# The S5 recurrence as rotations by tables around two scans, and the SSD gate's sums on another engine

## The chip, the cores and the metric

The program runs on one core of a Trainium2 chip. The metric is the device time of one execution in microseconds (us); the median of three runs counts. The profile is of one further execution of the same program. Engines: TensorE (PE) for matmuls, VectorE (DVE), ScalarE (ACT), GpSimd (POOL), and SyncE (SP), which issues most of the transfers. Each engine takes its instructions strictly in the order of its own queue and waits on semaphores for the others.

## The reference

The model has two blocks; the change is in the first, which has two layers (DEPTH = 2) with a mixer each, for 256 tokens of width 1024. A mixer projects its input, runs an SSD branch (chunks of 128 tokens, 32 heads) and an S5 branch, and merges them by gates. All is float32. The part that matters here is the S5 branch, a diagonal complex recurrence in 64 groups of 16 channels and 64 states:

```python
lam_bar = jnp.exp(lam * step)
b_bar = ((lam_bar - 1.0) / lam)[..., None] * lax.complex(b_re, b_im)
bu = jnp.einsum("blgc,gnc->blgn", ug.astype(jnp.complex64), b_bar)
_, states = lax.associative_scan(combine, (a_elems, bu), axis=1)   # s_t = lam_bar s_(t-1) + bu_t
y = jnp.real(jnp.einsum("blgn,gcn->blgc", states, c)).reshape(b, l, S5_WIDTH)
```

and the end of the SSD branch, which norms groups of 512 channels:

```python
yg = yg * lax.rsqrt(jnp.mean(yg * yg, axis=-1, keepdims=True) + RMS_EPS)
```

## The kernel before

The weights stream through numbered slots of 128x1024 (4 KB per partition). Each tile `raw` is split into two parts, `hi` by a cast on ScalarE (line 1517) and `lo` by a subtraction on VectorE (line 1518), and TensorE multiplies the parts in three products (lines 1532 to 1534). The order of the work of a mixer is written out in `mixer_body`: S5's input, its chunk states, then a list `ORDER` of units: projections (p), the step sizes (d, `ssd_dt`), SSD cores with their gates (c), branch gates (g) and S5's outputs by quarter (o). A scheduler then orders each engine's instructions by these units; what waits in a queue holds up what stands behind it.

S5 works on chunks of four tokens, 64 of them. 64 groups of 64 states are 32 pairs of groups with 128 states each, one state per partition. `s5_z` gives for every pair and chunk the state that the chunk's own tokens make; they lie in the tile `St`, [128, (re, im), pair, chunk]. `s5_rec` turns these into the states at each chunk's start, S_(c+1) = lambda^4 S_c + own_c. It runs on GpSimd, for half of the pairs at a time (h = 0, then h = 1). The 64 chunks are two runs of 32 that go at once: 31 steps of four small instructions (lines 505 to 509), each of 16 pairs x 2 runs x (re, im), and then the first run's end times lambda^(4i) into the second (lines 516 to 520), with a table E that `s5_powers_prep` (lines 276 to 278) makes for each layer on GpSimd and keeps in DRAM.

Quarter 0's output (o0, in `s5_y`, lines 454 to 456) and quarter 1's need half 0; quarters 2 and 3 need half 1. The products go to the one bank `z`, which ScalarE empties into `y` (line 465). Their table `s5CF` comes by a load on SyncE.

`ssd_dt` makes the step sizes by a chain of 32x256 instructions on VectorE, which ends in two scans (line 569); it writes the cumulated sums to DRAM (`acd`, line 573) and reads them back broadcast (`bc`, line 633). `ssd_core` makes of them the masks M (line 650), and TensorE multiplies M (lines 655 and 656). `ssd_gate` squares (line 670), adds the four 256-wide parts on GpSimd in two instructions (line 673), and TensorE adds over the partitions (line 675). There are four gates per mixer.

`s5_wb` makes the input table of each quarter by four instructions on GpSimd (lines 308 to 311); `s5_prep` of both layers stands ahead of the mixers, among the first block's other work.

Of the kernel before, what the change touches and what calls it, by code (L numbers as in the profile page):

```python
# [29 lines left out]
# the mixer's middle: projections and cores of the SSD's groups, steps, gates, outputs of S5  # L30
# [27 lines left out]
class Quads:  # L58
    """k-tiles [128, 256] held four to a tile."""
# [13 lines left out]
class Mixer:  # L73
    """Methods of Net for the first block's mixer."""

    def carver(self, tag="B"):
        """Small tiles cut from slots."""
        state = [None, 1024]

        def cut(n, p=P):  # L80
            if state[1] + n > 1024:
                state[0] = self.slot(tag, "cut")
                state[1] = 0
            a = state[0][:p, state[1] : state[1] + n]
# [46 lines left out]
    # ---- tables of both layers that come from the parameters alone  # L131
    def mix_prep(self, I):
# [27 lines left out]
        # masks: [s <= l | 1 | s <= l]  # L160
# [16 lines left out]
        # S5: [128 = (gi, n), (layer, pair)]  # L177
# [22 lines left out]

        cm0, cm1 = t("cm0"), t("cm1")
# [18 lines left out]
        # f = (lambda_bar - 1) / lambda  # L220
# [10 lines left out]
        # FL: f lambda^d as re, -im, -re  # L231
# [11 lines left out]
        # step of one chunk of four: re, (-im, im)  # L243
        self.L4r = ct.tile([P, NL], F32, name="L4r")
        self.L4i = ct.tile([P, 2, NL], F32, name="L4i")
        v.tensor_copy(self.L4r, L[4][0])
        v.tensor_scalar_mul(self.L4i[:, 0, :], L[4][1], -1.0)
        v.tensor_copy(self.L4i[:, 1, :], L[4][1])
        # lambda^(4-j), (gi, j), (layer, pair), (re | im, n), in DRAM
# [12 lines left out]
    def s5_powers_prep(self, l):  # L262
        """lambda^(4 i), i = 1..32, [128, pair, i], in DRAM"""
        nc = self.nc
        tt = nc.gpsimd.tensor_tensor
        E = [self.slot("B", "E").rearrange("p (a i) -> p a i", i=32) for _ in range(2)]
        Et = self.slot("B", "Et").rearrange("p (k a i) -> p k a i", k=2, i=16)
        x, y = Et[:, 0], Et[:, 1]
        ls = slice(l * 32, l * 32 + 32)
        nc.gpsimd.tensor_copy(E[0][:, :, 0], self.L4r[:, ls])  # L270
        nc.gpsimd.tensor_copy(E[1][:, :, 0], self.L4i[:, 1, ls])
        n = 1
        while n < 32:
            b = [e[:, :, n - 1 : n].to_broadcast([P, 32, n]) for e in E]
            for r, op in ((0, ALU.subtract), (1, ALU.add)):
                tt(x[:, :, :n], E[0][:, :, :n], b[r], op=ALU.mult)
                tt(y[:, :, :n], E[1][:, :, :n], b[1 - r], op=ALU.mult)
                tt(E[r][:, :, n : 2 * n], x[:, :, :n], y[:, :, :n], op=op)
            n *= 2
        self.Ed = self.dram.tile([2, P, 1024], F32, tag="Ed", name=self.nm("Ed"))  # L280
        for r in range(2):
            nc.gpsimd.dma_start(self.Ed[r], E[r].rearrange("p a i -> p (a i)"))
# [9 lines left out]
    def s5_wb(self, I, l, q):  # L292
        """lambda^(4-j) b, [(gi, j, c), (re, im), pair, n]"""
# [21 lines left out]
    def s5_ct(self, I, l, q):  # L315
        """c f lambda^d, rows for re and (negated) im of the state; the products within a chunk"""
# [65 lines left out]
    def s5_in(self, W, xh, xl):  # L382
        """u of 512 columns by features and (j, chunk), twice"""
# [21 lines left out]
    def s5_get(self, d):  # L405
        """U [(gi, j, c), pair, chunk]"""
# [8 lines left out]
    def s5_z(self, q, U, St):  # L415
        """the chunks' own contributions to the state"""
# [4 lines left out]
        for b in range(2):  # L421
            ps = self.zbank()
            for a4 in range(4):
# [22 lines left out]
        # [(gi, chunk), token of the chunk, (pair, c)]  # L446
# [12 lines left out]
    def s5_gelu(self, ps, gh, gl):  # L459
        """twice gelu (tanh form), back to features by tokens, [128 = (pair, c), gi, 256]"""  # L460
# [287 lines left out]
    def mixer_body(self, I, l, xh, xl, hd):  # L748
# [32 lines left out]
        for w in ORDER:  # L781
# [13 lines left out]
            elif k == "o":  # L795
                self.s5_out(i, U[i], St, g5)
# [1114 lines left out]
```

## Time and profile before

| | us |
|---|---|
| median of 3 runs | 2980.44 |
| lowest and highest run | 2979.87, 2983.41 |
| span of the profiled execution | 2978.5 |
| TensorE busy | 2823.1 |
| VectorE busy | 2101.8 |
| ScalarE busy | 1677.9 |
| GpSimd busy | 493.3 |
| mean granted clock of TensorE | 0.976 |

The profiled execution's own time is its span, from its first instruction to its last; the timed runs are other executions. A granted clock of 1.00 is 2.4 GHz, 0.5 is 1.2 GHz; a value between is a mean over a stretch. In rows of groups, "idle before" is the time in which the engine did nothing just before these instructions, with what ended it. In the names `out<-in` the buffer numbers are left out. Line numbers of instructions are those of the kernel before; the changed kernel's lines stand 3 to 15 higher.

### The profile page before, as it was taken

The page shows a single profiled execution, that of the slowest core. Times are in us where ns is not written, and L with a number is a line of the kernel's source. Part 1 is how long each engine was busy: PE and PEld are TensorE (multiplying, and loading weights), DVE is VectorE, ACT ScalarE, POOL GpSimd, SP SyncE. Part 2 cuts the span into 40 slices and gives each one's busy share as a digit, 9 for nine tenths or more (in the row PEclk, how much of TensorE's full clock was granted, in tenths as well). Part 3 has the DMA queues.
Part 4 walks back from the last instruction along what each step waited for, and adds up shares of the span by engine and source line. Part 5 has one row for each costly group of instructions (what it writes and reads, how often), then busy time and mean ns, then how long its engine had stood idle before and what let it go on. Part 6 is the DMA issues. An engine that isn't in the chain of part 4 may idle for free. (4 is left out here: it accounts for less than half of the span.)

```text
span 2978.5 us, 49449 instructions
## 1 busy us (share of the span) xinstructions
PE 2823.1 (95%) x19040; PEld 2513.6 (84%) x19040; DVE 2101.8 (71%) x2826; ACT 1677.9 (56%) x2381; POOL 493.3 (17%) x775
## 2 busy tenths in 40 slices
PE   8998879999998999699999999999999999999997
PEld 7877779999978889589989898987678888888885
DVE  6765756765557756567755566555589999999997
ACT  5334456545444445455554445444467777777776
POOL 2620891000006306940000000000000000000000
PEclk9999989999999999899999999999999999999998
DMA  7677535675556776355866656654579999999993
GB/s 234 204 225 241 156 105 178 229 226 178 184 182 219 224 238 184 118 167 164 275 192 180 202 163 191 185 184 142 170 269 351 351 355 365 344 357 358 355 341 142
DMA packets 351956, 679.53 MB, mean 228 GB/s; under 512 B 32416, under 2 KB 122720, under 8 KB 351712
## 3 DMA queue, kind: packets, MB, share of 16 engines
q1 hardware_dynamic: 344368, 652.10, 66.5%
q0 software_dynamic: 7200, 23.67, 2.2%
q8 instruction: 151, 2.47, 0.3%
q14 instruction: 93, 0.76, 0.1%
q10 hardware_dynamic: 144, 0.52, 0.0%
HBM read 653.86 MB, written 22.35 MB: 227 GB/s over the span
## 5 line engine op out<-in xcount | busy, mean ns | idle before, releaser
L1518 DVE TENSOR_TENSOR lo<-raw,hi 128x1024 fp32r<-128x1024 f32 x650 | 805.5, 1249 | 330.9 <-ACT hi L1517 321.9
L1517 ACT CAST hi<-raw 128x1024 fp32r<-128x1024 f32 x650 | 678.7, 1048 | 462.0 <-PE acc L1534 223.4
L1533 PE MATMUL acc<-xh,lo 128*128 128x256 f32 (+1 forms) x1656 | 475.3, 288 | 6.6 <-DVE lo L1518 6.6
L1532 PE MATMUL acc<-xh,hi 128*128 128x256 f32 (+1 forms) x1656 | 475.5, 289 | 5.4 <-ACT ht L1762 3.2
L1534 PE MATMUL acc<-xl,hi 128*128 128x256 f32 (+1 forms) x1656 | 472.4, 287 | 0.0
L1533 PEld LDWEIGHTS acc<-xh,lo 128*128 128x128 f32 (+1 forms) x1656 | 320.2, 193 | 10.4 <-DVE lo L1518 7.4
L1532 PEld LDWEIGHTS acc<-xh,hi 128*128 128x128 f32 (+1 forms) x1656 | 318.8, 193 | 11.8 <-ACT ht L1762 3.4
L1534 PEld LDWEIGHTS acc<-xl,hi 128*128 128x128 f32 (+1 forms) x1656 | 320.0, 194 | 1.4 <-issue 0.8
L1527 PE MATMUL acc<-lo,xg 128*128 128x512 f32 (+1 forms) x768 | 290.3, 378 | 1.9 <-DVE lo L1518 1.9
L1528 PE MATMUL acc<-hi,xg 128*128 128x512 f32 (+1 forms) x768 | 285.7, 373 | 0.0
L1526 PE MATMUL acc<-hi,xg 128*128 128x512 f32 (+1 forms) x768 | 274.6, 374 | 1.4 <-ACT hi L1517 1.4
L1518 DVE TENSOR_TENSOR big<-raw,big 128x1024 fp32r<-128x1024 f32 x147 | 191.4, 1306 | 106.7 <-ACT big L1517 106.3
L1517 ACT CAST big<-raw 128x1024 fp32r<-128x1024 f32 x147 | 153.8, 1049 | 171.1 <-PE acc L1534 65.5
L1518 DVE TENSOR_TENSOR part<-raw,part 128x1024 fp32r<-128x1024 f32 x107 | 131.2, 1231 | 93.1 <-ACT part L1517 90.8
L1686 POOL TENSOR_TENSOR sm<-sm,mhalf 128x1 f32<-128x1 f32 x32 | 19.7, 616 | 1043.9 <-DVE sm L1685 1043.7
L1517 ACT CAST part<-raw 128x1024 fp32r<-128x1024 f32 x107 | 111.9, 1050 | 119.5 <-PE acc L1534 33.2
L1527 PEld LDWEIGHTS acc<-lo,xg 128*128 128x128 f32 x768 | 144.9, 189 | 32.0 <-DVE lo L1518 5.2
L1526 PEld LDWEIGHTS acc<-hi,xg 128*128 128x128 f32 x768 | 144.8, 188 | 28.3 <-ACT hi L1517 2.6
L1528 PEld LDWEIGHTS acc<-hi,xg 128*128 128x128 f32 x768 | 145.0, 189 | 22.6
L1532 PE MATMUL acc<-xh,big 128*128 128x256 f32 x536 | 153.9, 287 | 2.2 <-DVE ht L1765 2.2
L1534 PE MATMUL acc<-xl,big 128*128 128x256 f32 x536 | 154.3, 288 | 0.0
L1533 PE MATMUL acc<-xh,big 128*128 128x256 f32 x536 | 154.0, 287 | 0.0
(552 smaller groups left out, 6994.7 us busy)
## 6 DMA issues: line engine op xcount, KB each, us to landing
raw<-in_w_gu_moe_dram SPq DMA_DIRECT2D x190, 512.0 KB, 5.6
raw<-in_w_in_dram SPq DMA_DIRECT2D x128, 512.0 KB, 4.0
raw<-in_w_down_moe_dram SPq DMA_DIRECT2D x94, 512.0 KB, 5.7
raw<-in_ffn_w_gate_dram SPq DMA_DIRECT2D x88, 512.0 KB, 3.9
raw<-in_ffn_w_up_dram SPq DMA_DIRECT2D x88, 512.0 KB, 4.1
raw<-in_ffn_w_down_dram SPq DMA_DIRECT2D x88, 512.0 KB, 3.7
big<-in_w_gu_moe_dram SPq DMA_DIRECT2D x60, 512.0 KB, 5.4
more<-in_w_gu_moe_dram SPq DMA_DIRECT2D x46, 512.0 KB, 5.5
```

Of the source, the lines that this page charges most:

```text
L1517: nc.scalar.copy(hi, raw)
L1518: nc.vector.tensor_tensor(lo, raw, hi.bitcast(F32), op=ALU.subtract)
L1526: mm(ps, lh, rh, start=first, stop=False)
L1527: mm(ps, lh, rl, start=False, stop=False)
L1528: mm(ps, ll, rh, start=False, stop=last)
L1532: mm(ps, lh, rh, start=first, stop=False)
L1533: mm(ps, ll, rh, start=False, stop=False)
L1534: mm(ps, lh, rl, start=False, stop=last)
L1686: self.last_pow = nc.gpsimd.tensor_tensor(r, v, self.mhalf, op=ALU.pow)
```

## The change

`s5_rec` no longer steps from chunk to chunk. With lambda^4 = r e^(i t), the own states are turned back by e^(-i t c), a real scan with the factor r runs over the chunks for the real and the imaginary part apart, and the result is turned forward again. Turning takes tables of cos and sin; r stands in a third table with 0 at each pair's first chunk, so that one scan runs through 16 pairs x 64 chunks = 1024 elements. For each half: three tables are loaded by SyncE, six GpSimd instructions of 128x1024 turn back, two scans run on VectorE, six GpSimd instructions turn forward. The tables' slots (E) are the same for both halves, and the temporaries x and y (W) lie in slots 2 and 3, which then go on to quarter 0's `y` and quarter 1's `s5CF`.

`s5_powers_prep` makes three tables of 16 pairs x 64 for each half (72 products per layer, before 30). `mix_prep` keeps r and e^(it) rather than lambda^4, with a correction of their length. `ssd_gate`'s two sums go to VectorE.

```diff
     def s5_powers_prep(self, l):
...
-        nc.gpsimd.tensor_copy(E[0][:, :, 0], self.L4r[:, ls])
-        nc.gpsimd.tensor_copy(E[1][:, :, 0], self.L4i[:, 1, ls])
-        n = 1
-        while n < 32:
-            b = [e[:, :, n - 1 : n].to_broadcast([P, 32, n]) for e in E]
...
+        for h in range(2):
+            E = [self.slot("B", "E").rearrange("p (a i) -> p a i", i=64) for _ in range(3)]
+            Et = self.slot("B", "Et").rearrange("p (k a i) -> p k a i", k=2, i=32)
...
+            g.memset(E[2][:, :, 0], 0.0)
+            g.tensor_copy(E[2][:, :, 1:], self.s4len[:, ls].unsqueeze(2).to_broadcast([P, 16, 63]))
...
+            for n in (1, 2, 4, 8, 16, 32):
+                k = min(n, 63 - n)
+                b = [e[:, :, n : n + 1].to_broadcast([P, 16, k]) for e in E[:2]]
+                for r, op in ((0, ALU.subtract), (1, ALU.add)):
+                    tt(x[:, :, :k], E[0][:, :, 1 : k + 1], b[r], op=ALU.mult)
+                    tt(y[:, :, :k], E[1][:, :, 1 : k + 1], b[1 - r], op=ALU.mult)
+                    tt(E[r][:, :, n + 1 : n + 1 + k], x[:, :, :k], y[:, :, :k], op=op)
+            for r in range(3):
+                g.dma_start(self.Ed[h, r], E[r].rearrange("p a i -> p (a i)"))
...
-    def s5_rec(self, St, l, h, E):
...
-        for s in range(1, 32):
...
-            tt(a, lr, Sv[:, :, :, g, s], op=ALU.mult)
-            tt(b, li, Sv[:, ::-1, :, g, s], op=ALU.mult)
-            tt(a, a, b, op=ALU.add)
...
-            tt(o, o, a, op=ALU.add)
...
+    def s5_rec(self, St, h):
         tt = self.nc.gpsimd.tensor_tensor
+        E = [self.slot("E", "s5E") for _ in range(3)]
+        for r in range(3):
+            self.nc.sync.dma_start(E[r], self.Ed[h, r])
+        c, s, m = E
+        x, y = (self.slot("W", "s5x") for _ in range(2))
+        re, im = (St[:, r, h * 16 : h * 16 + 16].rearrange("p a i -> p (a i)") for r in range(2))
+        tt(x, re, c, op=ALU.mult)
+        tt(y, im, s, op=ALU.mult)
+        tt(im, im, c, op=ALU.mult)
+        tt(re, re, s, op=ALU.mult)
+        tt(im, im, re, op=ALU.subtract)
+        tt(re, x, y, op=ALU.add)
+        for z in (im, re):
+            self.nc.vector.tensor_tensor_scan(z, m, z, 0.0, op0=ALU.mult, op1=ALU.add)
+        tt(x, re, c, op=ALU.mult)
+        tt(y, im, s, op=ALU.mult)
+        tt(im, im, c, op=ALU.mult)
+        tt(re, re, s, op=ALU.mult)
+        tt(im, im, re, op=ALU.add)
+        tt(re, x, y, op=ALU.subtract)
...
     def ssd_gate(self, l, g, yT, zs):
...
-            nc.gpsimd.tensor_tensor(sq[:, :n], sq[:, :n], sq[:, n : 2 * n], op=ALU.add)
+            v.tensor_tensor(sq[:, :n], sq[:, :n], sq[:, n : 2 * n], op=ALU.add)
```

The places at which the change moves work, in the first mixer:

On VectorE, before, in the middle of the projections that run beside the recurrence (cv is a convolution's sum, lo a weight's second part):

```order
L534 SCALAR_TENSOR_TENSOR cv_3071<-acc_2932,cw,cv_3071 128x253 [waits DVE_49]
L534 SCALAR_TENSOR_TENSOR cv_3684<-acc_3560,cw,cv_3684 128x254 [waits DVE_49]
L534 SCALAR_TENSOR_TENSOR cv_3684<-acc_3560,cw,cv_3684 128x253 [waits DVE_49]
L1518 TENSOR_TENSOR lo_3714<-raw_3712,hi_3713 128x1024 [waits DMAHW0_49,Activation_49]
L1518 TENSOR_TENSOR lo_3744<-raw_3742,hi_3743 128x1024 [waits DMAHW1_49,Activation_49]
L1518 TENSOR_TENSOR lo_3774<-raw_3772,hi_3773 128x1024 [waits DMAHW2_49,Activation_49]
```

And now, at the same place (S is St, s5E the table of factors):

```order
L537 SCALAR_TENSOR_TENSOR cv_3145<-accmx_3006,cw,cv_3145 128x253 [waits DVE_49]
L537 SCALAR_TENSOR_TENSOR cv_3406<-accpa_3282,cw,cv_3406 128x253 [waits DVE_49]
L517 SCALAR_TENSOR_TENSOR S_2762<-s5E_3162,S_2762 128x1024 [waits Pool_49]
L1530 TENSOR_TENSOR lo_3436<-raw_3434,hi_3435 128x1024 [waits DMAHW0_49,Activation_49]
L1530 TENSOR_TENSOR lo_3466<-raw_3464,hi_3465 128x1024 [waits DMAHW1_49,Activation_49]
L517 SCALAR_TENSOR_TENSOR S_2762<-s5E_3162,S_2762 128x1024 [waits Pool_49]
L1530 TENSOR_TENSOR lo_3496<-raw_3494,hi_3495 128x1024 [waits DMAHW2_49,Activation_49]
```

Half 0's two scans (line 517) stand among the splits, and the splits behind a scan wait with it for GpSimd.

On SyncE, before, around the step sizes' cumulated sums:

```order
L1512 DMA raw_4515<-in_w_in_dram 128x2x512 [waits DMAHW7_49,DVE_49]
L1512 DMA raw_4545<-in_w_in_dram 128x2x512 [waits DMAHW0_49,DVE_49]
L443 DMA s5T_5544<-Td_745 128x512 [waits PE_49]
L573 DMA acd_3905<-cut_3901 32x256 [waits DVE_49]
L633 DMA bc_4213<-acd_3905 128x512 [waits DMAHW6_49]
L633 DMA bc_4233<-acd_3905 128x512
```

And now:

```order
L458 DMA s5T_5266<-Td_762 128x512 [waits PE_49]
L1524 DMA raw_4177<-in_w_in_dram 128x2x512 [waits DMAHW0_49,DVE_49]
L1524 DMA raw_4207<-in_w_in_dram 128x2x512 [waits DMAHW1_49,DVE_49]
L457 DMA s5CF_4649<-Td_692 128x1024 [waits Pool_49]
L1524 DMA raw_4237<-in_w_in_dram 128x2x512 [waits DMAHW2_49,DVE_49]
L1524 DMA raw_4267<-in_w_in_dram 128x2x512 [waits DMAHW3_49,DVE_49]
L576 DMA acd_3627<-cut_3623 32x256 [waits DVE_49]
L636 DMA bc_3935<-acd_3627 128x512 [waits DMAHW2_49]
```

Quarter 1's table (s5CF) has moved down in the queue, to just ahead of acd, and waits for GpSimd, whose half 1 uses its slot.

On TensorE, before, at quarter 1's products (z is quarter 0's bank, then quarter 1's; tr the step sizes' transposes):

```order
L455 MATMUL z_4733<-s5CF_4729,S_2684 64x4x16
L456 MATMUL z_4733<-s5CF_4729,S_2684 64x4x16
L577 MATMUL tr_3907<-ident,cut_3901 128x32 [waits DVE_49]
L578 MATMUL tr_3907<-ident,cut_3871 128x32
L613 MATMUL tr_4195<-ident,xs_3558 128x128 x4
L577 MATMUL tr_3907<-ident,cut_3901 128x32 [waits DVE_49]
L578 MATMUL tr_3907<-ident,cut_3871 128x32
L454 MATMUL z_4931<-s5T_4928,U_2837 64x4x16 [waits PE_49,Activation_49]
```

And now (zob is quarter 1's bank, trda the step sizes'):

```order
L469 MATMUL zob_4653<-s5T_4650,U_2915 64x4x16 [waits PE_49,Activation_49]
L470 MATMUL zob_4653<-s5CF_4649,S_2762 64x4x16 [waits DMAHW7_49]
...
L469 MATMUL zob_4653<-s5T_4650,U_2915 64x4x16
L470 MATMUL zob_4653<-s5CF_4649,S_2762 64x4x16
L580 MATMUL trda_3629<-ident,cut_3623 128x32 [waits DVE_49]
L581 MATMUL trda_3629<-ident,cut_3593 128x32
```

Quarter 1's first products now stand ahead of the step sizes' transposes, and its second product waits for the load above.

## Rows read from the trace of the kernel before

**Rows 1.** page, part 1: busy time, share of the span, instructions of each engine

```profile
PE 2823.1 (95%) x19040; PEld 2513.6 (84%) x19040; DVE 2101.8 (71%) x2826; ACT 1677.9 (56%) x2381; POOL 493.3 (17%) x775
```

**Rows 2.** windows, first mixer: busy us (instructions), PEclk the granted clock, DMA share

```profile
300.00:320.00 20.00, 19.19 (x243) 18.05 (x242) 12.60 (x21) 12.72 (x21) 17.65 (x41) 1.00 0.46 133
320.00:340.00 20.00, 20.00 (x169) 19.65 (x168) 14.59 (x24) 10.22 (x17) 17.96 (x36) 1.00 0.63 190
340.00:360.00 20.00, 18.63 (x154) 18.23 (x153) 19.44 (x35) 7.82 (x9) 18.28 (x30) 1.00 0.46 131
360.00:380.00 20.00, 5.00 (x90) 4.79 (x90) 5.35 (x10) 1.04 (x1) 18.90 (x37) 0.61 0.29 100
```

**Rows 3.** waits of TensorE, first mixer: line, releaser: us in total, times, longest

```profile
PE z L455 <- POOL S L520: 15.0, 1, 15.0
PE tr L675 <- POOL zs L673: 9.4, 1, 9.4
...
PE tr L655 <- DVE M L650: 4.5, 1, 4.5
```

**Rows 4.** waits of TensorE, second layer's preparation and mixer

```profile
PE tr L675 <- POOL zs L673: 10.7, 1, 10.7
```

**Rows 5.** line 520, who waited for it: us in total, times

```profile
  PE z L455: 30.0, 2
```

**Rows 6.** groups by line, GpSimd: busy us, mean ns | idle before, releasers

```profile
L509 POOL TENSOR_TENSOR S<-S,ra 128x64 f32<-128x64 f32 (+1 forms) x124 | 66.0, 532 | 9.4
L505 POOL TENSOR_TENSOR ra<-L4r,S 128x64 f32<-128x64 f32 (+1 forms) x124 | 59.7, 481 | 69.6 <-ACT S L433 60.6
...
L308 POOL TENSOR_TENSOR s5t<-s5B,s5L 128x1024 f32<-128x1024 f32 x8 | 22.5, 2806 | 51.8 <-DMA Td<-s5u 30.6 <-DMA s5B<-in_s_bT_dram 17.1 <-DMA s5L<-lsd 4.1
...
L673 POOL TENSOR_TENSOR zs<-zs 128x512 f32<-128x512 f32 (+1 forms) x16 | 18.7, 1168 | 217.7 <-ACT zs L670 217.3
L278 POOL TENSOR_TENSOR E<-Et 128x32 f32<-128x32 f32 (+4 forms) x20 | 17.4, 870 | 1.2
```

**Rows 7.** timeline of GpSimd, 174 to 187 us: start, duration, instruction, idle before

```profile
174.81 2.39 POOL L308 TENSOR_TENSOR s5t<-s5B,s5L 128x1024 f32<-128x1024 f32 x1 [4.28 <-DMA Td<-s5u]
177.28 3.26 POOL L309 TENSOR_TENSOR s5B<-s5B,s5L 128x1024 f32<-128x1024 f32 x1
180.62 2.16 POOL L310 TENSOR_TENSOR s5B<-s5B,s5t 128x512 f32<-128x512 f32 x1
```

**Rows 8.** timeline of VectorE, 355 to 394 us, end of ssd_dt

```profile
364.65 0.84 DVE L569 TENSOR_TENSOR_SCAN cut<-ones,cut 32x128 f32<-32x128 f32 x2
381.98 0.43 DVE L466 TENSOR_SCALAR y<-y 128x512 f32<-128x512 f32 x1 [16.49 <-ACT y L465]
```

**Rows 9.** groups by line on VectorE, 560 to 880 us, outside preparation and mixer

```profile
L1518 DVE TENSOR_TENSOR lo<-raw,hi 128x1024 fp32r<-128x1024 f32 x51 | 62.2, 1223 | 43.4 <-ACT hi L1517 43.3
```

**Rows 10.** timeline of VectorE, 174 to 187 us, beside rows 7

```profile
174.93 3.35 DVE L1518 TENSOR_TENSOR big<-raw,big 128x1024 fp32r<-128x1024 f32 x1 [0.81 <-ACT big L1517]
178.20 3.41 DVE L1518 TENSOR_TENSOR lo<-raw,hi 128x1024 fp32r<-128x1024 f32 x1
```

**Rows 11.** groups by line on VectorE, 300 to 365 us, the first mixer

```profile
L1518 DVE TENSOR_TENSOR lo<-raw,hi 128x1024 fp32r<-128x1024 f32 (+1 forms) x15 | 18.0, 1202 | 11.6 <-ACT hi L1517 11.6
L534 DVE SCALAR_TENSOR_TENSOR cv<-acc,cw,cv 128x255 f32<-128x255 f32 (+2 forms) x33 | 13.8, 469 | 0.7 <-ACT cv L531 0.6
```

**Rows 12.** timeline of SyncE, 380 to 392 us

```profile
381.00 0.42 SPq L573 DMA_DIRECT2D acd<-cut  x1
```

**Rows 13.** PE's instructions of L655 and of L675: ns min/median/max, first start

```profile
L655 PE MATMUL tr<-M,xdt x128: 379/430/690, 393.7 to 1429.9; 128*64 128x256 f32 x128
...
L675 PE MATMUL tr<-ones,zs x32: 168/250/374, 427.6 to 1439.7; 128*128 128x1 f32 x32
```

**Rows 14.** windows of the preparations: layer 0, then layer 1

```profile
100.00:120.00 20.00, 12.86 (x77) 12.34 (x76) 12.17 (x8) 8.21 (x12) 18.31 (x18) 0.79 0.61 201
...
920.00:940.00 20.00, 15.96 (x119) 15.35 (x119) 19.93 (x21) 8.30 (x12) 15.24 (x13) 0.94 0.72 229
```

More of the change, by code (lines that the diff above doesn't have):

```diff
@@ L199, in mix_prep @@
         sn, cs = self.sincos32(cut, th, NL)
+        n2, n3 = t("n2"), t("n3")
+        v.tensor_tensor(n2, cs, cs, op=ALU.mult)
+        v.tensor_tensor(n3, sn, sn, op=ALU.mult)
+        v.tensor_tensor(n2, n2, n3, op=ALU.add)
+        v.tensor_scalar(n2, n2, -0.5, 1.5, op0=ALU.mult, op1=ALU.add)
+        v.tensor_tensor(cs, cs, n2, op=ALU.mult)
+        v.tensor_tensor(sn, sn, n2, op=ALU.mult)
         cm0, cm1 = t("cm0"), t("cm1")
@@ L242, in mix_prep @@
             v.tensor_scalar_mul(self.FL[:, 2, d, :], self.FL[:, 0, d, :], -1.0)
[L244 to L248, printed above, removed]
+        self.s4len = ct.tile([P, NL], F32, name="s4len")
+        self.s4dir = ct.tile([P, 2, NL], F32, name="s4dir")
+        u2 = t("u2r"), t("u2i")
+        cmul(*u2, (cs, sn), (cs, sn))
+        cmul(self.s4dir[:, 0], self.s4dir[:, 1], u2, u2)
+        v.tensor_tensor(mag, mag, mag, op=ALU.mult)
+        v.tensor_tensor(self.s4len, mag, mag, op=ALU.mult)
         lt = self.slot("B", "lt").rearrange("p (g j r n) -> p g j r n", j=4, g=2, r=2)[:NL]
@@ L262, in s5_powers_prep @@
     def s5_powers_prep(self, l):
[L264 to L269, printed above, removed]
-        nc.gpsimd.tensor_copy(E[0][:, :, 0], self.L4r[:, ls])
-        nc.gpsimd.tensor_copy(E[1][:, :, 0], self.L4i[:, 1, ls])
-        n = 1
-        while n < 32:
-            b = [e[:, :, n - 1 : n].to_broadcast([P, 32, n]) for e in E]
[L275 to L279, printed above, removed]
@@ L280, in s5_powers_prep @@
-        self.Ed = self.dram.tile([2, P, 1024], F32, tag="Ed", name=self.nm("Ed"))
-        for r in range(2):
-            nc.gpsimd.dma_start(self.Ed[r], E[r].rearrange("p a i -> p (a i)"))
+        g = self.nc.gpsimd
+        tt = g.tensor_tensor
+        self.Ed = self.dram.tile([2, 3, P, 1024], F32, tag="Ed", name=self.nm("Ed"))
+        for h in range(2):
+            E = [self.slot("B", "E").rearrange("p (a i) -> p a i", i=64) for _ in range(3)]
+            Et = self.slot("B", "Et").rearrange("p (k a i) -> p k a i", k=2, i=32)
+            x, y = Et[:, 0], Et[:, 1]
+            ls = slice(l * 32 + h * 16, l * 32 + h * 16 + 16)
+            g.memset(E[2][:, :, 0], 0.0)
+            g.tensor_copy(E[2][:, :, 1:], self.s4len[:, ls].unsqueeze(2).to_broadcast([P, 16, 63]))
+            for r in range(2):
+                g.memset(E[r][:, :, 0], 1.0 - r)
+                g.tensor_copy(E[r][:, :, 1], self.s4dir[:, r, ls])
+            for n in (1, 2, 4, 8, 16, 32):
[7 more added lines that the diff above has]
+                g.dma_start(self.Ed[h, r], E[r].rearrange("p a i -> p (a i)"))
@@ L796, in mixer_body @@
                 self.s5_out(i, U[i], St, g5)
+        self.at = "gl"
         bs = self.glu(I["s5_w_glu"][l], g5)
+        self.at = "mb"
         ys += [self.ssd_split(y) for y in y23]
```

66 lines of the change are left out of this document (23 added, 43 removed).

## The prediction

> **What bounds the kernel now.** I read the page's first part, then the windows of 20 us, then the waits of TensorE, then the single instructions on GpSimd and VectorE. TensorE is busy 95% of the span and GpSimd 17% [rows 1], so the change can give only what TensorE loses in the few places where it waits for GpSimd. There are two per mixer. In the windows of the first mixer TensorE works 19 to 20 us of 20 until 360, and then 5.00 us of 20 at a granted clock of 0.61 [rows 2]: one wait of 15.0 us, of quarter 0's output products (line 455) for the last instruction of the recurrence (line 520). Later the column sums of the first gate wait 9.4 us for GpSimd's sum (line 673), because that instruction stands behind the recurrence of half 1; 4.5 us go to the decay masks [rows 3]. The second mixer repeats it with 15.0 (30.0 for both mixers) and 10.7 us [rows 4, 5]. That is 28.9 us of waits in the first mixer and about as much in the second, and nothing else that this change touches is worth more.
>
> The reader should look at VectorE in the same windows: 12.60, 14.59 and 19.44 us of 20 until 360 [rows 2]. It is nearly full just ahead of the wait. There the change puts larger instructions on GpSimd, and the argument hangs on what those do to VectorE.
>
> **What goes.** Line 505 to line 509 are four groups of 124 small instructions, the costliest 66.0 us and the first 59.7 us [rows 6]; with the fix-ups they fill 17.65 to 18.90 us of each window of 20 [rows 2]. From 300 us they take 75 us per half, which is why half 0 ends at 375. They go, and so does the wait of 15.0 us at its present place.
>
> **What comes, alone.** Per mixer 24 GpSimd instructions of 128x1024 and four scans on VectorE. The nearest row is line 308, a product of the same shape: 2.39 us where nothing is beside it [rows 7], 2.81 on average [rows 6]. The trace has no scan of 1024 elements. The scan of 32x128 takes 0.42 us each (0.84 for two) [rows 8]; by elements alone that is 3.4 us, less if part of the 0.42 is fixed, and as a plain two-input instruction it would be 1.22 [rows 9]. I take 2.4, bounds 1.2 and 3.4. Undisturbed, half 0 is then done after 12 x 2.4 + 2 x 2.4 = 34 us, at about 334, when TensorE still has work until 360.
>
> **What comes, beside VectorE.** The two engines work in turns [rows 7, 10]. GpSimd runs 174.81 to 177.20; VectorE's split, issued at 174.93, takes 3.35 us rather than 1.22; GpSimd's next, from 177.28, takes 3.26 rather than 2.39; VectorE's next takes 3.41. Each waits out the other's whole instruction. Small ones don't show this: between 300 and 365 the split takes 1.20 us [rows 11], against 1.22 elsewhere [rows 9], although GpSimd is over 90% busy. So the new form has about as many elements to process as the old, but in pieces that hold VectorE up for over 2 us each. VectorE's instructions that read PSUM, such as the convolution's (line 534, 13.8 us [rows 11]), I count as undisturbed.
>
> The Trainium skill's page "SBUF — State Buffer", section "Who interferes with whom", has a rule for this: a VectorE instruction with two SBUF inputs contends with a GpSimd instruction that reads SBUF, and issue order decides who blocks. It speaks against this change; the trace agrees with it by the 1.22 to 3.41 us above. "GPSIMD Engine Reference", section "4.1 Engine selection", advises VectorE for two-input elementwise work, where GpSimd is about twice as slow; the rows say 1.22 against 2.39. By that page the 24 instructions would be 29 us on VectorE, rather than 55 on GpSimd that both wait for.
>
> The budget of turns for the first mixer: VectorE has 12.60 + 14.59 + 19.44 + 5.35 = 52.0 us from 300 to the end of the step sizes' chain (ssd_dt) at 365.5 [rows 2, 8]. Less 13.8 that read PSUM leaves 38. GpSimd brings 24 x 2.3 = 55 (2.39 less about 0.1 that isn't held), the scans 4 x 2.4 = 10. Together 103 us, so 403 if the two never overlap. Stepping through VectorE's new order instruction by instruction, each side waiting for the other's current one, I get: scan 1 at 314, half 0 done at 341, half 1 at 389, ssd_dt's chain done at 398. With scans of 1.3 it is 394, with scans of 3.4 and 2.4 per product about 404. Splits reach TensorE late by 20 to 25 us in sum by then, which is a wait that wasn't there: it replaces the 15.0.
>
> **What waits then.** Quarter 0 is ready (341 against TensorE's arrival at 360 plus the delay). Quarter 1's table load shares its slot with half 1's temporary, and on SyncE it stands ahead of the load and broadcast of the cumulated steps (acd, bc), which the decay masks need. Both conditions end late: half 1 at 389, the chain at 398. Before, acd was issued at 381.0 [rows 12] and the first masked product (line 655) ran at 393.7 [rows 13], 12.7 us later. Now 398 + 12.7 = 411. From there to the column sums it was 427.6 - 9.4 - 393.7 = 24.5 us [rows 3, 13]; the sums are on VectorE now, which has half of that stretch free, and wait for nothing. 411 + 24.5 = 435.5, against 427.6: 8 us later. After the wait of 9.4 the matmuls ran at the lower clock for a while (a column sum takes 168 to 374 ns [rows 13]); I estimate 2 us, which don't recur, so +6 for this mixer. The second has the same order and 10.7 rather than 9.4: +5. Together +11.
>
> **The tables' preparation.** Per layer 72 small GpSimd products rather than 30, up to 496 elements, and four more stores of 512 KB. At the mean of 870 ns of line 278 [rows 6] the 42 more are at most 37 us, and copies add some 5; I take 30, since most are shorter than those of before. They stand between the four input products of a layer (line 323, 308 before), with gaps of some us ahead of each (51.8 us over 8 [rows 6]), so that most fits without delaying them. But TensorE already loses 7.1 and 4.0 us in the windows where the present tables are made, while VectorE is busy 19.93 of 20 in the second [rows 14]. If turns cost there what they cost in the mixer, 30 us could be 20; if they hit gaps, nothing. I take +2 per layer, bounds 0 and +10. The extra VectorE instructions of the constants (about 20 of 128x64) are under 5 us in all, beside loads at the start: 0, bound +2. The gate sums on VectorE: 16 instructions of 512 and 256 elements, 0.6 us and less by the 1.22 for 1024 [rows 9], where it is idle: 0. The two to four extra table loads per mixer (512 KB each) fall into windows with a DMA share of 0.46 to 0.63 [rows 2]; the weights behind them on SyncE wait up to 8 us for half 0's end, which the weight buffers ahead cover; without that cover it would be +8 per mixer.
>
> **Sum.** +11 +4 = +15 on the profiled span of 2978.5 us; the median of the runs is 1.9 us above that span, so 2995.
>
> **The rivals.**
> A, no turns that matter: VectorE's instructions fall between GpSimd's. For it: VectorE has gaps (12.6 and 14.6 of 20 until 340 [rows 2]), and the small instructions cost it nothing. Then half 1 ends at about 368, the load of quarter 1's table takes 4 more, TensorE waits 6 to 8 us there, and line 655 runs at 382 rather than 393.7; with the 9.4 gone this gives 21 per mixer, and with +2 of preparation per layer -38 to -40: 2941. Against it: [rows 7, 10], and the window 340 to 360, which has no gaps.
> B, turns in part: VectorE slips by 10 us rather than 25, because the scans take 1.3 and GpSimd waits in the queue gaps. Line 655 at about 396, sums' wait gone: -5 per mixer, +2 to +4 of preparation: -4 in all, 2976.
> C, the turns decide fully and the preparation pays as well: chain at 404, +13 per mixer, and the 30 us of new products at the start of each layer stall saturated VectorE for +8: +42, 3022. It decides from the point where VectorE has no gap left from 900 to 960.
> D, the change moves the wait but no time: quarter 1 now waits for half 1 by the shared slot as long as quarter 0 did, and the gates' 9 to 10 us are what remains as gain, eaten by the preparation: within 6 us, 2980.
>
> **How the numbers follow.** The forecast (2986 to 3008) has 0.32; A 0.30; B and D 0.21, of which 0.13 inside the bound and 0.08 below; C 0.17. What a measurement can tell from no change is 0.2%, about 6 us. Faster by more is A and part of B: 0.38. Within is part of B and D: 0.13. Slower is the forecast and C: 0.49. The range holds A's centre and C: 2936 to 3026; the forecast's own is 2986 to 3008.
>
> **What would show it.** In the profile after: the product of 128x1024 near 2.4 us alone and over 3 beside VectorE; splits of 3 us and more between 300 and 390; the scan's duration; line 470 without its 15 us wait, but TensorE waiting for splits (lo) by 20 us in sum; acd issued at about 398; the column sums without a wait. If the splits stay at 1.2 us, A is right and my sum fails at its first step. If acd leaves before 381, the forecast is wrong even with long splits.

## The result

| | us |
|---|---|
| before, median of 4 runs | 2980.15 (2975.0 to 2983.41) |
| after, median of 4 runs | 2997.36 (2994.32 to 3004.73) |
| ratio, with its 95% interval | 1.0071 [1.0054, 1.0088] |
| span of the profiled execution after | 2994.0 (before 2978.5) |

The change is slower by 0.7%. TensorE has the same 19,040 matmuls; GpSimd does less than before [rows 1], VectorE more:

```profile
PE 2839.2 (95%) x19040; PEld 2527.7 (84%) x19040; DVE 2186.4 (73%) x2867; ACT 1671.3 (56%) x2377; POOL 398.0 (13%) x383
```

### The profile after, first mixer

The windows from 320 on, as in [rows 2], then 380 to 400 and 420 to 440 of the kernel before, which were not shown:

```profile
320.00:340.00 20.00, 15.47 (x146) 14.60 (x145) 17.12 (x15) 7.26 (x14) 16.48 (x6) 1.00 0.34 94
340.00:360.00 20.00, 17.70 (x144) 17.34 (x143) 18.61 (x10) 9.56 (x12) 19.69 (x8) 0.96 0.63 200
360.00:380.00 20.00, 11.76 (x113) 10.35 (x112) 19.86 (x21) 1.61 (x2) 9.77 (x5) 0.61 0.29 82
380.00:400.00 20.00, 11.87 (x85) 11.26 (x85) 19.61 (x27) 5.17 (x6) 10.36 (x4) 0.82 0.34 103
...
420.00:440.00 20.00, 20.00 (x165) 18.73 (x164) 17.02 (x32) 15.46 (x34) 0.72 (x1) 1.00 0.75 228
```

```profile
380.00:400.00 20.00, 15.45 (x132) 13.11 (x129) 14.61 (x30) 16.74 (x39) 17.96 (x37) 0.80 0.36 107
...
420.00:440.00 20.00, 12.37 (x103) 11.63 (x104) 6.01 (x16) 6.20 (x12) 17.64 (x48) 0.74 0.24 72
```

VectorE is busy 18.61 to 19.86 us of 20 for 60 us on end. TensorE loses 4.5 us already at 320 to 340, where it lost nothing, works 11.76 rather than 5.00 at 360 to 380, and 11.87 rather than 15.45 at 380 to 400. At 420 to 440 the order is the other way round: TensorE works 20.00 us at full clock, where before it worked 12.37 at a mean of 0.74.

TensorE's waits, first and second mixer, answering to [rows 3, 4]:

```profile
PE accpb L1545 <- DVE lo L1530: 10.0, 4, 4.6
PE accpa L1545 <- DVE lo L1530: 6.0, 4, 1.6
...
PE zob L470 <- DMA s5CF<-Td: 3.4, 1, 3.4
...
PE trca L658 <- DVE M L653: 1.8, 1, 1.8
```

```profile
PE zob L470 <- DMA s5CF<-Td: 8.2, 1, 8.2
PE accpb L1545 <- DVE lo L1530: 7.3, 4, 2.4
```

The waits for the recurrence and for the column sums are gone. In their place stand waits for splits (lo, 16.0 us in the first mixer's two rows) and for quarter 1's table load.

Now the instructions themselves, GpSimd and then VectorE, from their timelines (start, duration). The first four GpSimd rows are of half 1's turning back, the last is half 1's end:

```profile
346.64 3.27 POOL L510 TENSOR_TENSOR s5x<-S,s5E 128x1024 f32<-128x1024 f32 x1
349.87 3.39 POOL L511 TENSOR_TENSOR s5x<-S,s5E 128x1024 f32<-128x1024 f32 x1
...
355.74 3.57 POOL L512 TENSOR_TENSOR S<-S,s5E 128x1024 f32<-128x1024 f32 x1
359.39 2.37 POOL L514 TENSOR_TENSOR S<-S 128x1024 f32<-128x1024 f32 x1
...
388.20 2.39 POOL L523 TENSOR_TENSOR S<-s5x,s5x 128x1024 f32<-128x1024 f32 x1
```

```profile
347.57 3.43 DVE L1530 TENSOR_TENSOR part<-raw,part 128x1024 fp32r<-128x1024 f32 x1
...
353.57 2.35 DVE L97 TENSOR_SCALAR cut<-cut 32x256 f32<-32x256 f32 x1
355.85 1.20 DVE L1530 TENSOR_TENSOR lo<-raw,hi 128x1024 fp32r<-128x1024 f32 x1
...
364.83 1.20 DVE L1530 TENSOR_TENSOR lo<-raw,hi 128x1024 fp32r<-128x1024 f32 x1
...
369.61 2.27 DVE L517 TENSOR_TENSOR_SCAN S<-s5E,S 128x1024 f32<-128x1024 f32 x1
```

A GpSimd instruction takes 2.37 to 2.39 us where it does not wait for VectorE, and 3.27 to 3.57 where it does. The split at 347.57 takes 3.43 us; the one at 355.85 has its turn first and takes 1.20, and the GpSimd instruction beside it, issued at 355.74, takes the 3.57. At 364.83 GpSimd stands still, and the split takes 1.20 too. The row at 353.57 is an instruction of the step sizes' chain with one input, 32x256; it took 2.35 us, and its likes 0.27 to 0.28 at 366, where GpSimd stood still. The scan of 1024 elements takes 2.27 us.

Two of SyncE's transfers, the load of quarter 1's table and the store of acd, and the first start of the masked products (line 658) and of the column sums (line 678), answering to [rows 12, 13]:

```profile
396.05 0.46 SPq L457 DMA_DIRECT2D s5CF<-Td  x1
...
402.33 0.34 SPq L576 DMA_DIRECT2D acd<-cut  x1
```

```profile
L658 PE MATMUL trca<-M,xdt x32: 379/430/689, 416.6 to 1275.7; 128*64 128x256 f32 x32
```

```profile
L678 PE MATMUL trca<-ones,zs x8: 168/250/250, 436.7 to 1284.8; 128*128 128x1 f32 x8
```

acd leaves at 402.3, the masked products start at 416.6 and the column sums at 436.7.

### The profile page after: what moved, and what is told of

Its sections match the earlier page's. It is cut to its first block, busy times and chain, and to the rows that moved or that the text cites. A ratio compares the mean times of both kernels' runs of the same rounds, so it can differ in the third digit from the quotient of the medians.

```text
span 2994.0 us, 49128 instructions
## 1 busy us (share of the span) xinstructions
PE 2839.2 (95%) x19040; PEld 2527.7 (84%) x19040; DVE 2186.4 (73%) x2867; ACT 1671.3 (56%) x2377; POOL 398.0 (13%) x383
## 5 line engine op out<-in xcount | busy, mean ns | idle before, releaser
L1539 PE MATMUL accmo<-lo,xg 128*128 128x512 f32 (+1 forms) x768 | 290.3, 378 | 2.2 <-DVE lo L1530 2.2
L1540 PE MATMUL accmo<-hi,xg 128*128 128x512 f32 (+1 forms) x768 | 285.7, 373 | 0.0
L1538 PE MATMUL accmo<-hi,xg 128*128 128x512 f32 (+1 forms) x768 | 274.5, 374 | 1.4 <-ACT hi L1529 1.4
L1539 PEld LDWEIGHTS accmo<-lo,xg 128*128 128x128 f32 x768 | 144.9, 189 | 32.3 <-DVE lo L1530 5.5
L1538 PEld LDWEIGHTS accmo<-hi,xg 128*128 128x128 f32 x768 | 144.7, 188 | 28.3 <-ACT hi L1529 2.6
L1540 PEld LDWEIGHTS accmo<-hi,xg 128*128 128x128 f32 x768 | 145.0, 189 | 22.5
L1539 PE MATMUL accmo<-lo,th 128*128 128x512 f32 x352 | 138.0, 392 | 0.0
L1540 PE MATMUL accmo<-hi,th 128*128 128x512 f32 x352 | 137.7, 391 | 0.0
L1530 DVE TENSOR_TENSOR lo<-big,hi 128x1024 fp32r<-128x1024 f32 x88 | 106.6, 1224 | 10.6 <-ACT hi L1529 7.2
L1538 PE MATMUL accmo<-hi,th 128*128 128x512 f32 x352 | 109.1, 391 | 0.0
L1544 PE MATMUL accfa<-xh,hi 128*128 128x256 f32 x352 | 103.6, 295 | 5.2 <-ACT ht L1774 3.1
L1545 PE MATMUL accfa<-xh,lo 128*128 128x256 f32 x352 | 103.6, 294 | 1.3 <-DVE lo L1530 1.3
L1546 PE MATMUL accfa<-xl,hi 128*128 128x256 f32 x352 | 103.0, 293 | 0.0
```

The source lines that it names most:

```text
L1530: nc.vector.tensor_tensor(lo, raw, hi.bitcast(F32), op=ALU.subtract)
L1538: mm(ps, lh, rh, start=first, stop=False)
L1539: mm(ps, lh, rl, start=False, stop=False)
L1540: mm(ps, ll, rh, start=False, stop=last)
L1544: mm(ps, lh, rh, start=first, stop=False)
L1545: mm(ps, ll, rh, start=False, stop=False)
```

## The lag of TensorE

All kernels here run 19,040 matmuls in nearly the same order. So the start of the n-th matmul in one trace less its start in the trace before says how late TensorE is at that point of the work. This table is worked out from the traces; its first column is the time in the trace before, the others are lags in us.

| at | change | slots apart | pieces | no products | on VectorE | memsets | half 1 late | late, on VectorE | tables too |
|---|---|---|---|---|---|---|---|---|---|
| 299, first mixer's start | 3.6 | -0.2 | 2.2 | -13.7 | -2.1 | -0.2 | 1.4 | 0.7 | 0.5 |
| 350 | 20.0 | 15.7 | 10.2 | 2.1 | 0.8 | -2.3 | 6.6 | 6.3 | 7.9 |
| 400 | 12.5 | 1.6 | 15.2 | -3.5 | -8.7 | -23.0 | -17.0 | -20.5 | -19.5 |
| 440 | 3.6 | -2.0 | 6.8 | -12.6 | -16.6 | -29.5 | -3.4 | -15.1 | -13.4 |
| 520, its end | 4.3 | 0.8 | 2.8 | -11.4 | -11.6 | -25.9 | -3.3 | -13.0 | -8.4 |
| 850 | 4.3 | 0.9 | 2.8 | -11.7 | -11.5 | -26.3 | -3.4 | -13.4 | -8.4 |
| 1140, second mixer's start | 10.9 | 7.4 | 11.1 | -18.5 | -4.6 | -18.6 | 3.7 | -3.9 | -12.5 |
| 1400, its end | 11.3 | 6.4 | 14.5 | -18.3 | -18.2 | -43.8 | -1.0 | -15.2 | -27.4 |
| 2900 | 14.8 | 5.1 | 13.7 | -19.5 | -18.0 | -40.5 | -0.5 | -15.2 | -27.0 |

Two executions of one preparation differ. Nine traces have the same instructions up to 299: seven of the table, all but "no products" and "tables too", and two that it leaves out, of the pieces with slots apart and of the change with the gates' sums put back. Their lags there go from -2.1 to 8.6, with a mean of 2.1. So differences under some 10 us in one row of this table, from one trace to another, are not told from chance.

## The experiments

Each was timed beside the kernel before, so the ratio is what is compared; 0.0010 is 3 us.

### Slots of their own for half 1's temporaries

```diff
-    "E": [10, 11, 14], "W": [2, 3],
+    "E": [10, 11, 14], "W": [2, 3, 6, 7],
```

> The change, with half 1's temporaries x and y in slots of their own (6 and 7), so that quarter 0's evacuation and quarter 1's table load no longer wait for half 1. Theory T (GpSimd's long instructions hold VectorE up, and the step sizes' chain, done at 402 us, is what comes last): the table load leaves SyncE's queue earlier, but acd still leaves at about 400, so line 658 moves by 0 to 2 us in the first mixer and by up to 5 in the second; total 0 to 8 us less than the change, about 2993. Rival S (the shared slots are what hold TensorE between 374 and 404): quarter 1 runs right behind quarter 0, some 15 to 20 us per mixer go, total about 2960.

Ratio 1.0048 [1.0031, 1.0064], against 1.0071 for the change: some 7 us less, with intervals that overlap. TensorE's waits in the first mixer:

```profile
PE trda L580 <- DVE cut L572: 2.2, 1, 2.2
```

Quarter 1's wait for its load is gone, and TensorE waits for the step sizes' chain (line 580) right behind it instead; acd leaves at 398.1. That is theory T's 0 to 8 us. The shared slots were not what cost; rival S expected 2960.

### Rotations in pieces, with and without slots apart

```diff
-        tt = self.nc.gpsimd.tensor_tensor
+        def tt(o, p, q, op):
+            for k in range(0, 1024, 128):
+                w = slice(k, k + 128)
+                self.nc.gpsimd.tensor_tensor(o[:, w], p[:, w], q[:, w], op=op)
```

> The change, with each of the 24 rotation instructions per mixer cut into 8 of 128x128 on GpSimd; slots as in the change. Theory T: a split on VectorE waits for at most one piece (about 0.4 us), so splits beside the recurrence fall from over 3 us to under 1.7; TensorE's waits for splits between 300 and 380 fall from some 19 us to under 8 and the step sizes' chain ends near 375 rather than 402. GpSimd's halves end later (half 1 past 400). Total 10 to 25 us less than the change, about 2980. Rival U (the scans on VectorE and the table loads on SyncE delay the splits, not the rotations): splits and waits as in the change, total as the change or slower, 2997 to 3010, since 192 instructions cost more in sum than 24.

> Both edits: pieces of 128x128 and slots of their own for half 1. Theory T: with VectorE no longer held up, the shared slots come last, so together they give more than the sum of the two alone: 20 to 40 us less than the change, 2955 to 2975. Rival S: as with slots alone. Rival U: as with slots alone, or slower.

Ratios 1.0071 [1.0058, 1.0084] and 1.0054 [1.0041, 1.0067]: no gain, against theory T. The splits did get short after 310, as T says and against rival U, and yet the chain ended late. The timelines with pieces alone, VectorE and then GpSimd (start, duration, idle before):

```profile
297.20 9.42 DVE L1534 TENSOR_TENSOR lo<-raw,hi 128x1024 fp32r<-128x1024 f32 x2 [3.17 <-ACT hi L1533]
310.21 1.23 DVE L1534 TENSOR_TENSOR part<-raw,part 128x1024 fp32r<-128x1024 f32 x1 [3.59 <-ACT part L1533]
...
376.94 5.42 DVE L521 TENSOR_TENSOR_SCAN S<-s5E,S 128x1024 f32<-128x1024 f32 x1 [8.83 <-POOL S L506]
382.28 0.39 DVE L562 TENSOR_TENSOR cut<-cut,cut 32x256 f32<-32x256 f32 x1
```

```profile
376.88 3.33 POOL L506 TENSOR_TENSOR S<-s5x,s5x 128x128 f32<-128x128 f32 x8
382.50 5.47 POOL L506 TENSOR_TENSOR s5x<-S,s5E 128x128 f32<-128x128 f32 x1 [2.30 <-DVE S L521]
```

Half 1's first scan stands in VectorE's queue ahead of the rest of the step sizes' chain. It waits 8.83 us for GpSimd, which with 8 pieces for one is now the slow side, and then takes 5.42 us rather than 2.27, beside the 8 pieces of the last instruction of turning back (the row at 376.88); the chain's next instruction starts at 382.28 and acd leaves at 396.7, where T had 375. TensorE waits 18.5 us for it. So what was taken from the splits came back as a wait of a queue. The row at 297.20 is a surprise of its own, below.

### The gates' sums, alone and undone

On the kernel before, the sums alone moved:

```diff
-            nc.gpsimd.tensor_tensor(sq[:, :n], sq[:, :n], sq[:, n : 2 * n], op=ALU.add)
+            v.tensor_tensor(sq[:, :n], sq[:, :n], sq[:, n : 2 * n], op=ALU.add)
```

> The kernel before, with only the gates' sums moved to VectorE; the recurrence steps as before. Theory T (the sums' wait of 9.4 and 10.7 us is worth what it shows, and some us of lower clock behind it): the column sums wait for nothing, the power behind them still stands in GpSimd's queue; 8 to 25 us less than the kernel before, about 2965. Rival V (the wait only moves to the power, which stands behind the recurrence): within 5 us of the kernel before.

Ratio 0.9982 [0.9971, 0.9993], 5 us faster, at the edge between the two. The wait at the column sums is gone, and a new one stands at the next product (line 685), behind GpSimd's power, first and second mixer:

```profile
PE tr L685 <- DVE dg L684: 8.5, 1, 8.5
```

```profile
PE tr L685 <- DVE sm L638: 14.4, 1, 14.4
```

VectorE in the second mixer, on the way to that product:

```profile
1277.69 0.33 DVE L684 TENSOR_SCALAR dg<-ident,sm 128x128 f32<-128x128 f32 x1 [17.16 <-POOL sm L680]
```

The 9.4 and 10.7 us went mostly to the instruction behind, as rival V says. In the change itself, with the same line put back (the diff above the other way round):

> The change with only the gates' sums put back on GpSimd. Theory T (in the change GpSimd is idle from about 390, before the first gate's sums at 435, so their engine no longer matters): the sums add some 1 us to each gate's chain, hidden or not, total 0 to 6 us more than the change, about 3000. Rival G (the sums' move carries a gain of its own, as it did on the kernel before): 8 us or more slower than the change.

Ratio 1.0049 [1.0036, 1.0061], not slower than the change (1.0071): rival G is out, and theory T's 0 to 6 us more did not come either. The sums' engine doesn't matter once GpSimd is idle. Of the two edits in the change, the sums' move is worth nothing beside the other. The change's ratio rests on four runs; this run and the one with the slots apart, which do nearly the same work, both stand at 1.005, so the change's 1.0071 may be some us high.

### The tables without their products

The loop that fills cos and sin is left out, and all three tables are cleared instead.

```diff
-            for n in (1, 2, 4, 8, 16, 32):
...
+            for r in range(3):
+                g.memset(E[r], 0.0)
```

> The change without the 72 products per layer that fill the tables of cos and sin (the tables are zeros; the six stores per layer stay). It leaves that part of the computation out and prices the preparation. Theory T (the preparation is what remains of the loss: TensorE is 3.6 us later at the start of the first mixer and 6.6 us later between the mixers): 6 to 12 us less than the change, about 2988, and the lag of TensorE does not grow between 880 and 1140 us. Rival Q (the preparation fits the gaps, and the loss is the mixers'): within 3 us of the change.

Ratio 0.9951 [0.9935, 0.9966]: 0.0120, or 36 us, less than the change, where 6 to 12 were expected. By the lag table 17 of them lie ahead of the first mixer (3.6 against -13.7) and 13 between the mixers (+6.6 against -6.8). This is the price of the whole tables, those of the kernel before included, which had 30 products per layer. Splits on VectorE from 900 to 960, in the change, without the products, and with the products and the sums back on GpSimd:

```profile
L1530 DVE TENSOR_TENSOR lo<-raw,hi 128x1024 fp32r<-128x1024 f32 x10 | 26.5, 2660 | 9.3 <-ACT hi L1529 9.3
```

```profile
L1517 DVE TENSOR_TENSOR lo<-raw,hi 128x1024 fp32r<-128x1024 f32 x11 | 15.4, 1414 | 2.8 <-ACT hi L1516 2.8
```

```profile
L1530 DVE TENSOR_TENSOR lo<-raw,hi 128x1024 fp32r<-128x1024 f32 x12 | 17.0, 1428 | 9.4 <-ACT hi L1529 9.3
```

They take 2.66 us in the change and 1.41 without the products. But the 2.66 comes from one split of 12.03 us, shown in the last section; the other nine take 1.62 on average. In the third row the same products run, the splits take 1.43, and TensorE still loses 8.8 us between the mixers. So the price of the tables is shown, but not that it is paid by the splits' waiting.

### Rotations on VectorE

```diff
-        tt = self.nc.gpsimd.tensor_tensor
+        tt = self.nc.vector.tensor_tensor
```

> The change with the 24 rotation instructions per mixer on VectorE rather than GpSimd. Theory T: on VectorE alone they take about 1.22 us each, 29 us instead of 55 that both engines wait for; from 300 us VectorE then has 38 + 14 + 29 + 10 = 91 us of work and the step sizes' chain ends near 393 to 398 rather than 402, so little is gained: 0 to 12 us less than the change, about 2991. Rival R (VectorE is full there, so any work put on it costs its whole length): later than the change by 10 us or more.

Ratio 0.9976 [0.9965, 0.9987]: 28 us less than the change and faster than the kernel before; T had 0 to 12. Each rotation takes what a split takes:

```profile
L510 DVE TENSOR_TENSOR s5x<-S,s5E 128x1024 f32<-128x1024 f32 x4 | 4.9, 1223 | 0.6 <-ACT S L448 0.6
```

acd leaves at 386.8, earlier than 393 to 398. In the first mixer TensorE waits 0.5 us for splits; what is left are waits for the chain (6.9) and for convolution sums (9.3). Rival R fell clearly: 29 us more work on the busiest engine of that stretch gained time, because it took away the rotations on GpSimd, 72 us per mixer with their waits, beside which VectorE waited as well.

### Memsets in place of the rotations

The 24 rotations per mixer are replaced by memsets of the same tiles on GpSimd, which write and read nothing.

```diff
-        tt(x, re, c, op=ALU.mult)
...
+        for o in (x, y, im, re, im, re):
+            ms(o, 1.0)
```

> The change with each of the 24 rotations per mixer replaced by a GpSimd memset of the same 128x1024 result, which reads nothing; scans, loads and slots as in the change. It leaves the rotations out. Theory T (it is GpSimd's reading of SBUF against VectorE's second input): splits beside the memsets stay near 1.22 us, whatever the memsets last, and the step sizes' chain ends by 380; 10 to 25 us less than the change, about 2980. Rival N (any long GpSimd instruction holds VectorE up): splits beside the memsets take up to a memset's length more.

Ratio 0.9896 [0.9875, 0.9916]. Groups by line: the memsets, the splits beside them (305 to 375 us), and the same splits in the change:

```profile
L515 POOL MEMSET S<- 128x1024 f32 x8 | 7.6, 952 | 7.9 <-DVE S L513 7.7
```

```profile
L1522 DVE TENSOR_TENSOR lo<-raw,hi 128x1024 fp32r<-128x1024 f32 (+1 forms) x14 | 16.3, 1161 | 8.6 <-ACT hi L1521 8.6
```

```profile
L1530 DVE TENSOR_TENSOR lo<-raw,hi 128x1024 fp32r<-128x1024 f32 (+1 forms) x11 | 22.4, 2053 | 3.9 <-ACT hi L1529 3.9
```

That is 52 us less than the change, where theory T had 10 to 25. A memset takes 0.95 us and the splits 1.16, against 2.05 in the change; rival N's wait of up to a memset's length is not there. acd leaves at 372.6. Scans, loads and slots stand as in the change, so they are not what cost. The memsets are shorter than the rotations, so the 52 us are not a price of the turns alone; that the splits don't feel them at all speaks for GpSimd's reading, as the Trainium skill's page "SBUF — State Buffer", section "Who interferes with whom", has it (a GpSimd instruction that only writes is no rival of VectorE's second input).

### Half 1 behind the step sizes' chain

With slots apart, `self.s5_rec(St, 1)` is moved into the list of units and ordered behind the chain's last scan and the store acd.

```diff
-        self.s5_rec(St, 1)
...
                 proj(i)
+                if i == 1:
+                    with self.tc.issue_after(self.dt_end.ins), self.tc.issue_after(self.dt_out.ins):
+                        self.s5_rec(St, 1)
```

> The change with all of half 1's recurrence (loads, rotations, scans) ordered behind the step sizes' chain and its store acd, and with slots of their own for half 1's temporaries. Same work. Theory T (what costs is where the long instructions stand: half 1 is needed only by quarter 2's products at about 469 us): the step sizes' chain ends near 375 rather than 402, TensorE's waits for splits fall to half, quarter 2 is not delayed; 15 to 35 us less than the change, about 2972, below the kernel before. Rival M (VectorE is as full after 400, so the delay only moves): within 8 us of the change.

Ratio 1.0013 [1.0, 1.0025], 17 us less than the change: at the lower end of theory T's 15 to 35, but not below the kernel before, and more than rival M's 8. acd leaves at 375.4, as expected, and then a part of the delay moves, as rival M says. TensorE's waits from 300 to 560, and VectorE's timeline:

```profile
PE trca L658 <- DVE M L653: 17.0, 3, 11.9
```

```profile
413.91 6.12 DVE L653 TENSOR_TENSOR M<-M,cb 128x768 f32<-128x768 f32 x2
419.95 6.68 DVE L1532 TENSOR_TENSOR lo<-raw,hi 128x1024 fp32r<-128x1024 f32 x2
```

Two masks (line 653, 128x768) take 6.12 us together, against 1.83 at 415.48 in the change, where GpSimd was done; two splits take 6.68. TensorE waits 17.0 us for M. The long GpSimd instructions now hold up the masks and the splits beside them; later is cheaper, not free.

### Late on VectorE, and the tables there too

The edits of the sections on VectorE and on half 1 together, slots apart, with half 1 emitted behind unit c0 rather than p1:

```diff
-        tt = self.nc.gpsimd.tensor_tensor
+        tt = self.nc.vector.tensor_tensor
...
+                if i == 0:
+                    with self.tc.issue_after(self.dt_end.ins), self.tc.issue_after(self.dt_out.ins):
+                        self.s5_rec(St, 1)
```

> The change with all rotations on VectorE, half 1's whole recurrence ordered behind the step sizes' chain and its store, and slots of their own for half 1's temporaries. Same work. Theory T (no long GpSimd instruction is left beside VectorE, and half 1 is due only at quarter 2, some 90 us later): acd leaves near 375, splits and masks keep their undisturbed durations, half 1's 14 instructions (19 us) fill VectorE between the masks; 8 to 20 us less than with the rotations on VectorE alone, about 2960, clear below the kernel before. Rival M (VectorE has no room between the masks either, as it had none with half 1 late on GpSimd): the wait for M returns with 10 us or more per mixer, total as with the rotations on VectorE alone or slower, 2972 or more.

And with the tables' products on VectorE as well, in `s5_powers_prep`:

```diff
-        tt = g.tensor_tensor
+        tt = self.nc.vector.tensor_tensor
```

> As the run with half 1 late on VectorE, and the 72 products per layer that fill the tables go to VectorE as well. Theory T (the products hold VectorE up by turns while they run on GpSimd: leaving them out gave 33 us): on VectorE they are some 17 us per layer in its queue without turns, at places where it is nearly full, so a part of the 33 comes back: 0 to 15 us less than that run. Rival R (VectorE is full in the preparation, each microsecond put on it is late): 10 us or more slower than that run.

With half 1 late and all rotations on VectorE: ratio 0.9971 [0.9961, 0.9981], no different from rotations on VectorE alone (0.9976); the 8 to 20 us didn't come. acd leaves at 377.0, but the lags show what is won by 420 (-27.9) given back by 470 (-12.1; with all rotations on VectorE alone -16.5 and -18.7). TensorE's waits:

```profile
PE accpc L1547 <- DVE lo L1532: 5.7, 4, 2.4
PE accpa L1546 <- DVE cv L537: 4.8, 2, 4.0
```

The waits for M did not come back, but rival M's premise holds. From 400 to 420 VectorE is full, from 400 to 440 TensorE waits 7.9 us for splits and for a convolution's sum, and its granted clock falls:

```profile
410.00:420.00 10.00, 7.36 (x33) 5.18 (x33) 10.00 (x16) 1.80 (x5) 0.00 (x0) 0.51 0.61 177
420.00:430.00 10.00, 6.96 (x43) 6.87 (x42) 7.90 (x15) 7.24 (x14) 0.00 (x0) 0.63 0.01 5
```

Half 1's rotations, which stand from 382.6 to 425.3 between masks and splits, take their 1.2 us each, but what stands behind them in VectorE's queue is late by them.

With the tables' products there too: ratio 0.9907 [0.9894, 0.9920], 2949.5 us against 2978.4. That is 19 us less than the run with half 1 late alone, where theory T had 0 to 15, and it beats both kernels. Between the mixers the lag now falls by 4.1 us, where it grew by 9.5; ahead of the first mixer the products' move gains nothing (0.5 against 0.7). One of the five groups of products, and the page:

```profile
L295 DVE TENSOR_TENSOR E<-Et 128x16 f32<-128x16 f32 (+5 forms) x48 | 17.4, 368 | 0.2
```

```profile
PE 2823.5 (96%) x19040; PEld 2514.6 (85%) x19040; DVE 2176.9 (74%) x3059; ACT 1677.5 (57%) x2383; POOL 163.2 (6%) x191
```

The products take 368 ns on VectorE rather than 772, and GpSimd is down to 163 us. Rival R fell again.

## Why the prediction was right, and where it wasn't

The forecast was 2995, the median is 2997.4. The mechanism in the mixers held; the terms of the sum did not, and that the total came out so near is luck.

- **Turns between the two engines.** Right, and shown: 2.37 us without a wait and 3.3 with one, splits of over 3 us, and these gone with memsets and with the rotations on VectorE. Rival A fell at its first step. (The forecast has GpSimd over 90% busy with the small instructions; by [rows 2] it is 88 to 91%, and nothing hangs on it.)
- **The scan.** Taken at 2.4, measured 2.27.
- **The chain.** Half 1's end at 389 (390.6), ssd_dt's end and acd at 398 (402.3), line 658 at 411 (416.6), column sums at 435.5 without a wait (436.7). The recurrence began 6 us later than before (306.1 against 299.7), which the forecast had not put in; the stretches themselves were some us shorter.
- **The term of the mixers, +6 and +5, is the mis-sized one.** Over a whole mixer the lag grew by 0.7 us (3.6 to 4.3) and by 0.4 (10.9 to 11.3). The step that failed is the last: I counted 24.5 us from line 658 to the column sums and 2 us of lower clock. The column sums did start 9.1 us later (436.7 against 427.6), but that is not TensorE's lag: counted in the traces, TensorE had started 34 more matmuls by then than at the same point before (2901 against 2867), and 53 more at line 658 (2735 against 2682), since its queue had done other work of that stretch meanwhile. At the same matmul the lag was 5.0 us at 427 and fell to 3.6 by 440: before, TensorE stood until 427.6 and ran on in that window at a mean clock of 0.74.
- **The preparation, +2 per layer with a bound of +10.** In this execution 3.6 ahead of the first mixer and 6.6 between the mixers. Over the nine traces with the same preparation the first is 2.1 on average, as forecast, with the spread named above; the second goes from 3.6 to 9.5, on average 7.2, and there the forecast was too low. The products took 105.8 us for both layers against 51.0, 27 more per layer (30 were taken). That they cost by turns was not shown. One group of them:

```profile
L295 POOL TENSOR_TENSOR E<-Et 128x16 f32<-128x16 f32 (+5 forms) x48 | 36.5, 772 | 0.7
```

- **3.5 us** of the lag come between 2000 and 2200, in the second block, which the change does not touch. With memsets there are 3.3 from 1400 to 2900, in the other traces -1.3 to 0.8, so this may be chance; it stays open.

So in this execution 1 + 10 + 4 gave what 11 + 4 was to give: the mixers' term was too high by about as much as the rest was too low. By these traces the sign rests on the preparation, of the second layer above all, and not on the mixers, where the change moved the waits and broke even. The advice of the Trainium skill's page "GPSIMD Engine Reference", section "4.1 Engine selection", was worth more than the forecast gave it: with the rotations on VectorE the runs are 28 us shorter than the change's, and with half 1 late and the tables there too they are 0.9% under the kernel before.

## What to carry to other kernels

An engine that is 83% idle is not free help if each of its instructions holds up a full one: price an instruction on GpSimd by what VectorE waits for it as well, in its own windows, and try the work on the fuller engine. When a wait is removed by longer instructions, look at the instructions that read beside them and at the queue of the engine that must take the result. Sum up the lag of TensorE at several points of the program: a total that fits can hide two wrong terms.

## What the runs showed of the hardware

Turns are not always one for one. In the change itself one split waited out a whole chain on GpSimd, ten instructions back to back in the second layer's preparation (the first and the last of them are shown):

```profile
955.30 12.03 DVE L1530 TENSOR_TENSOR lo<-raw,hi 128x1024 fp32r<-128x1024 f32 x1
```

```profile
955.22 0.65 POOL L293 TENSOR_TENSOR Et<-E 128x256 f32<-128x256 f32 x1
...
965.52 0.72 POOL L295 TENSOR_TENSOR E<-Et 128x256 f32<-128x256 f32 x1
```

With the slots apart and with the pieces the same split took 12.05 and 12.03 us; in the other traces with the same preparation it did not, though in four of them another instruction of a preparation took 7.8 to 14.7 us. With pieces of 128x128, until its wait that ends at 310.73, GpSimd ran its pieces back to back at 0.43 us each, and two splits took 9.42 us (the row at 297.20 above); the next four pieces took 0.82 us each and the splits beside them their usual 1.23. At 382.50 it was GpSimd that waited: one piece took 5.47 us (its row stands with the pieces' section), while VectorE ran five instructions back to back, from the scan at 382.60 on, and its splits took 1.21. GpSimd's timeline:

```profile
299.39 1.71 POOL L506 TENSOR_TENSOR s5x<-S,s5E 128x128 f32<-128x128 f32 x4
...
310.73 3.28 POOL L506 TENSOR_TENSOR s5x<-S,s5E 128x128 f32<-128x128 f32 x4 [6.33 <-ACT S L448]
```

What decides which of the two sides yields was not settled by these runs. A scan of 128x1024 takes 2.27 us, 1.9 times a plain instruction of its size.
